# A row softmax on one core: the last two rows of the sixth tile's load move from Sync to GpSimd, behind a wait

## The chip, the cores and the metric

The kernel runs on one core of one Trainium2 chip. Time is the device time of one launch in microseconds; before the change it is 162.26 us, the median of three runs (162.25 to 162.98). Alongside stands one profiled execution, from which all durations below come.

## The reference

A softmax over the last axis of a float32 tensor of 16 x 1024 rows of 512 elements, at temperature 0.5:

```python
x_scaled = x / 0.5
x_max = np.max(x_scaled, axis=-1, keepdims=True)
exp_x = np.exp(x_scaled - x_max)
return exp_x / np.sum(exp_x, axis=-1, keepdims=True)
```

There are 16384 rows: 33.55 MB are read and 33.55 MB written.

## The kernel before, in words

**Tiles.** The rows are cut into eight tiles of 128 partitions x 16 rows x 512 elements (4 MB each). A partition's 16 rows lie next to each other in memory, so each partition's share of a tile is one run of 32 KB. Tiles are counted here as in the code, c = 0 to 7; "the sixth tile" is c = 5, "the fourth" c = 3. Six buffers hold tiles (`BUFS = 6`); tile 6 reuses the buffer of tile 0, tile 7 that of tile 1. Everything is done in place: the load writes the buffer, the exponentials overwrite it, the scaling overwrites it again, and the store reads it.

**Blocks.** Work on tiles goes by blocks (`BLOCKS`). Tile 0 is three blocks (rows 0-3, 4-7, 8-15), tiles 1 to 6 are one block each, tile 7 is two. So blocks 0, 1, 2 are tile 0, block 3 is tile 1, block 4 is tile 2, block 5 is tile 3, block 6 is tile 4, block 7 is tile 5, and there are eleven in all. `biases[5]` are therefore the biases of the fourth tile.

**Stages of a block.**
- `shift`: VectorE takes the negated maximum of each row (`tensor_reduce`, line 74) and doubles it (line 78); that is the bias. If the tile has no load yet, `shift` calls `load` first.
- `exponentials`: ScalarE computes exp(2x + bias) row by row, with the row's sum as a second output (line 85).
- `scale_vector`: VectorE takes the reciprocals of the sums (line 100) and multiplies seven eighths of the rows by them (line 102).
- `scale_scalar`: ScalarE scales the remaining eighth (line 111).
- `store`: ScalarE issues the store of the whole tile (line 119) after its last block.

**Order.** The order of each engine's instructions is the order in which the code calls them (`manual_schedule`). The main loop at lines 126 to 133 runs, for block i: exponentials of i+1, scaling of i, shift of i+2, store of i. So on VectorE the maximum of a block stands between the scaling of the block two before it and the scaling of the block one before it: the maximum of tile 5 (block 7) comes after the scaling of tile 3 (block 5) and before the scaling of tile 4 (block 6).

**Queues.** All loads are issued by Sync (line 66), in order of tiles. The first six tiles have a buffer of their own, so Sync issues their loads one after another at the start without a wait (the last, tile 5's, at 3.79 us). The loads of tiles 6 and 7 wait for the stores of tiles 0 and 1. All stores are issued by ScalarE. GpSimd has no work of the kernel. Waits between engines and on loads are put in from the buffers that instructions read and write.

Of the kernel before, what the change touches and what calls it, by code (L numbers as in the profile page):

```python
# [1 line left out]

# [4 lines left out]


@with_exitstack
def kernel(  # L10
    ctx: ExitStack,
    tc: tile.TileContext,
    x: bass.AP,
    out: bass.AP,
):
    nc = tc.nc
    fp32 = mybir.dt.float32
    P = nc.NUM_PARTITIONS
    AX = mybir.AxisListType.X
    EXP = mybir.ActivationFunctionType.Exp  # L20
    COPY = mybir.ActivationFunctionType.Copy
    MAX = mybir.AluOpType.max

    D = x.shape[-1]
    xf = x.flatten_outer_dims()
    of = out.flatten_outer_dims()
    N = xf.shape[0]

    G = 16
    C = N // (P * G)
    assert C * P * G == N
    xr = xf.rearrange("(c p g) d -> c p g d", p=P, g=G)
    outr = of.rearrange("(c p g) d -> c p g d", p=P, g=G)
    WHOLE = [(0, G)]
    LOADS = [[(0, 4), (4, G)]] + [WHOLE] * 7
    BLOCKS = [[(0, 4), (4, 8), (8, G)]] + [WHOLE] * 6 + [[(0, 8), (8, G)]]
    STORES = [WHOLE] * 8  # L40
    BMAX = 16
    BUFS = 6

    data = ctx.enter_context(tc.tile_pool(name="data", bufs=BUFS))
    stats = ctx.enter_context(tc.tile_pool(name="stats", bufs=6))

    ctx.enter_context(tc.manual_schedule())


    warm = stats.tile([P, 1], fp32, name="warm", bufs=1)  # L50
    nc.vector.memset(warm, 0.0)  # L51
    nc.scalar.activation(out=warm, in_=warm, func=EXP)  # L52

    chunks = {}
    blocks = [(c, lo, hi) for c in range(C) for lo, hi in BLOCKS[c]]
    n = len(blocks)
    biases, sums, recips = {}, {}, {}

    def load(c):
        if c < BUFS:  # L60
            chunks[c] = data.tile([P, G, D], fp32, name="xt")
        else:
            chunks[c] = chunks[c - BUFS]
        xt = chunks[c]
        for lo, hi in LOADS[c]:
            nc.sync.dma_start(out=xt[:, lo:hi, :], in_=xr[c][:, lo:hi, :])  # L66

    def shift(i):
        c, lo, hi = blocks[i]
        if c not in chunks:  # L70
            load(c)
        b = hi - lo
        negmax = stats.tile([P, BMAX], fp32, name="negmax")
        nc.vector.tensor_reduce(  # L74
            negmax[:, 0:b], chunks[c][:, lo:hi, :], axis=AX, op=MAX, negate=True
        )
        biases[i] = stats.tile([P, BMAX], fp32, name="bias")
        nc.vector.tensor_scalar_mul(biases[i][:, 0:b], negmax[:, 0:b], 2.0)  # L78

    def exponentials(i):  # L80
        c, lo, hi = blocks[i]
        sums[i] = stats.tile([P, BMAX], fp32, name="sums")
        for g in range(hi - lo):
            row = chunks[c][:, lo + g, :]
            nc.scalar.activation(  # L85
                out=row,
                in_=row,
                func=EXP,
                bias=biases[i][:, g : g + 1],
                scale=2.0,  # L90
                accum_out=sums[i][:, g : g + 1],
            )


    def scale_vector(i):
        c, lo, hi = blocks[i]
        b = hi - lo
        k = b - b // 8
        recips[i] = stats.tile([P, BMAX], fp32, name="recip")
        nc.vector.reciprocal(recips[i][:, 0:b], sums[i][:, 0:b])  # L100
        rows = chunks[c][:, lo : lo + k, :]
        nc.vector.tensor_mul(  # L102
            rows, rows, recips[i][:, 0:k].unsqueeze(2).broadcast_to((P, k, D))
        )

    def scale_scalar(i):
        c, lo, hi = blocks[i]
        b = hi - lo
        for g in range(b - b // 8, b):
            row = chunks[c][:, lo + g, :]  # L110
            nc.scalar.activation(  # L111
                out=row, in_=row, func=COPY, scale=recips[i][:, g : g + 1]
            )

    def store(i):
        c, _, end = blocks[i]
        for lo, hi in STORES[c]:
            if hi == end:
                nc.scalar.dma_start(
                    out=outr[c][:, lo:hi, :], in_=chunks[c][:, lo:hi, :]  # L120
                )

    shift(0)
    shift(1)
    exponentials(0)
    for i in range(n):
        if i + 1 < n:
            exponentials(i + 1)
        scale_vector(i)
        scale_scalar(i)  # L130
        if i + 2 < n:
            shift(i + 2)
        store(i)


# [1 line left out]
_INS = ['x']  # L137
_OUTS = [((16, 1024, 512), 'float32')]


# [23 lines left out]
```

## Time and profile before

| what | value |
|---|---|
| median of 3 runs | 162.26 us |
| profiled execution | 162.34 us |
| its span | 160.6 us |
| VectorE (DVE) busy | 134.6 us, 84% |
| ScalarE (ACT) busy | 102.1 us, 64% |
| GpSimd (POOL) busy | 0.2 us |
| mean DMA rate over the span | 418 GB/s |
| time to landing of the loads of tiles 0 to 5 | 4.9 and 11.7 (tile 0 in two pieces), up to 71.8 us (tile 5) |
| time to landing of a store, median | 22.8 us |

The span runs from the first to the last instruction that the profile shows; the rest of the time lies around it. A row of forty digits shows the busy share of forty equal slices of a stretch, in tenths. DMA queue q1 is Sync's, q10 ScalarE's, q14 the fetching of instructions. "Time to landing" is from the issue of a DMA to its last byte's arrival. A wait line reads: the engine, tile and line that waited, what it waited for, microseconds in total, how often, the longest. In lists in order of time the first two columns are start and duration in microseconds, and square brackets give idle time before an instruction and what ended it.

### The profile page before, as it was taken

To read this page: it belongs to the slowest core of one execution; us is meant where nothing else is said; L and a number is where in the kernel's file an instruction comes from. 1 tells how busy PE (TensorE), PEld (TensorE's weight loads), DVE (VectorE), ACT (ScalarE), POOL (GpSimd) and SP (SyncE) were. 2 spreads that over 40 slices of the span, in tenths; PEclk is the share of its full clock that TensorE was granted. 3 is DMA by queue.
4 is the path that set the end of the run, shared out by engine and by line. 5 is a ranking of instruction groups with operands and counts; after the bars stand their busy time and mean duration, and the time that the engine had idled before them with its cause. 6 is when DMAs were issued, how large, how long until landed. Compare 5 with 4: busy or idle time off the path is not lost.

```text
span 160.6 us, 402 instructions
## 1 busy us (share of the span) xinstructions
DVE 134.6 (84%) x45; ACT 102.1 (64%) x273; POOL 0.2 (0%) x4
## 2 busy tenths in 40 slices
DVE  0507999999999999999999999999999999957000
ACT  3071549069979963998199909991899891790000
POOL 0000000000000000000000000000000000000000
DMA  5999999999999999999999999999999999999993
GB/s 182 471 400 506 400 400 498 408 392 484 424 400 384 400 457 449 400 441 465 400 424 473 408 408 492 400 392 498 416 392 490 424 392 457 457 392 449 465 392 139
DMA packets 2450, 67.13 MB, mean 418 GB/s; under 512 B 272, under 2 KB 272, under 8 KB 272
## 3 DMA queue, kind: packets, MB, share of 16 engines
q1 hardware_dynamic: 1296, 33.56, 49.3%
q10 hardware_dynamic: 1152, 33.55, 48.4%
q14 instruction: 2, 0.02, 0.0%
HBM read 33.55 MB, written 33.55 MB: 418 GB/s over the span
## 4 chain that ended last, share of the span: by engine, by line
DVE 80%; DMA 7%; ACT 4%; issue 0%; SPq 0%
DVE negmax L74 42%; DVE xt L102 36%; DMA xt<-in_x_dram 7%; ACT xt L85 4%; DVE bias L78 1%; DVE recip L100 1%; SPq L66 0%
## 5 line engine op out<-in xcount | busy, mean ns | idle before, releaser
L85 ACT ACTIVATE xt<-xt,bias 128x512 f32<-128x512 f32 x128 | 90.4, 708 | 41.7 <-DVE bias L78 41.2
L74 DVE TENSOR_REDUCE negmax<-xt 128x16 f32<-128x8192 f32 (+2 forms) x11 | 69.9, 6352 | 9.5 <-DMA xt<-in_x_dram 9.5
L102 DVE TENSOR_TENSOR xt<-xt,recip 128x7168 f32<-128x7168 f32 (+2 forms) x11 | 62.0, 5637 | 0.4
L85 ACT ACTIVATION_READ_ACCUMULATOR xt<-xt,bias 128x1 f32 x128 | 23.9, 187 | 0.0
L111 ACT ACTIVATE xt<-xt,recip 128x512 f32<-128x512 f32 x15 | 9.9, 706 | 0.0
L100 DVE RECIPROCAL recip<-sums 128x16 f32<-128x16 f32 (+2 forms) x11 | 2.4, 218 | 1.8 <-ACT xt L85 1.8
L78 DVE TENSOR_SCALAR bias<-negmax 128x16 f32<-128x16 f32 (+2 forms) x11 | 1.9, 173 | 0.4
L52 ACT ACT_TABLE_LOAD x1 | 1.3, 1283 | 0.7 <-PEq L148 0.7
L51 DVE MEMSET warm<- 128x1 f32 x1 | 0.1, 59 | 0.8 <-PEq L148 0.8
L52 ACT ACTIVATE warm<-warm 128x1 f32<-128x1 f32 x1 | 0.2, 203 | 0.0
L148 POOL MEMSET const-bfloat16-1.0<- 128x1 bf16 x1 | 0.1, 103 | 0.0
L148 POOL MEMSET const-uint8-127<- 128x1 uint8 x1 | 0.1, 103 | 0.0
L148 POOL MEMSET const-float32-1.0<- 128x1 f32 x1 | 0.1, 100 | 0.0
L148 POOL MEMSET const-float32-0.0<- 128x1 f32 x1 | 0.1, 99 | 0.2 <-issue 0.2
## 6 DMA issues: line engine op xcount, KB each, us to landing
out_dram<-xt ACTq DMA_DIRECT2D x8, 4096.0 KB, 22.8
xt<-in_x_dram SPq DMA_DIRECT2D x7, 4096.0 KB, 30.2
xt<-in_x_dram SPq DMA_DIRECT2D x1, 3072.0 KB, 11.7
xt<-in_x_dram SPq DMA_DIRECT2D x1, 1024.0 KB, 4.9
```

Source lines behind the costliest of these rows:

```text
L51: nc.vector.memset(warm, 0.0)
L52: nc.scalar.activation(out=warm, in_=warm, func=EXP)
L74: nc.vector.tensor_reduce(negmax[:, 0:b], chunks[c][:, lo:hi, :], axis=AX, op=MAX, negate=True)
L78: nc.vector.tensor_scalar_mul(biases[i][:, 0:b], negmax[:, 0:b], 2.0)
L85: nc.scalar.activation(out=row, in_=row, func=EXP, bias=biases[i][:, g : g + 1], scale=2.0, accum_out=sums[i][:, g : g + 1],)
L100: nc.vector.reciprocal(recips[i][:, 0:b], sums[i][:, 0:b])
L102: nc.vector.tensor_mul(rows, rows, recips[i][:, 0:k].unsqueeze(2).broadcast_to((P, k, D)))
L111: nc.scalar.activation(out=row, in_=row, func=COPY, scale=recips[i][:, g : g + 1])
L148: nc = _bacc.Bacc("TRN2", target_bir_lowering=False, num_devices=1)
```

## The change

For the sixth tile alone (`SPLIT = 5`), Sync's load covers rows 0 to 13 of each partition. The last two rows (`TAIL = 2`) of all 128 partitions, 0.5 MB, are loaded by GpSimd instead, in two DMAs: partitions 126 and 127 first, then partitions 0 to 125. Ahead of them GpSimd copies one column of `biases[5]`, the biases of the fourth tile, into a small tile that nothing reads; since GpSimd works in order, its two DMAs are issued only after those biases exist. `max_dma_last_dim` limits the contiguous last dimension of a transfer; it is a number of bytes, here 4 x 512 = 2048, one row. Sync's loads are not held by any of this.

```diff
     STORES = [WHOLE] * 8
+    SPLIT, TAIL = 5, 2
+    HOLD = 5
     BMAX = 16
...
         xt = chunks[c]
         for lo, hi in LOADS[c]:
+            if c == SPLIT and hi == G:
+                hi = G - TAIL
+                hold = stats.tile([P, 1], fp32, name="hold", bufs=1)
+                nc.gpsimd.tensor_copy(hold, biases[HOLD][:, 0:1])
+                for p0, p1 in ((P - 2, P), (0, P - 2)):
+                    nc.gpsimd.dma_start(
+                        out=xt[p0:p1, hi:G, :],
+                        in_=xr[c][p0:p1, hi:G, :],
+                        max_dma_last_dim=4 * D,
+                    )
             nc.sync.dma_start(out=xt[:, lo:hi, :], in_=xr[c][:, lo:hi, :])
```

## The prediction

> **What bounds the kernel now.** I read the head of the page first: engines, the row of the DMA engines, the queues, the chain.
>
> ```profile
> span 160.6 us, 402 instructions
> DVE 134.6 (84%) x45; ACT 102.1 (64%) x273; POOL 0.2 (0%) x4
> DMA  5999999999999999999999999999999999999993
> ...
> q1 hardware_dynamic: 1296, 33.56, 49.3%
> q10 hardware_dynamic: 1152, 33.55, 48.4%
> q14 instruction: 2, 0.02, 0.0%
> ...
> DVE negmax L74 42%; DVE xt L102 36%; DMA xt<-in_x_dram 7%; ACT xt L85 4%; DVE bias L78 1%; DVE recip L100 1%; SPq L66 0%
> ```
>
> Two things are full at once. The sixteen DMA engines are busy 97.7% of the span (49.3 + 48.4), and the chain is VectorE from 12.88 us to 147.48 us. Neither can be lengthened for nothing, so I asked each for its slack. The waits from 13 us on hold nothing of a load after the second piece of tile 0; in order of time, around the change's two moments (the fourth tile's biases, the sixth tile's maximum):
>
> ```profile
> 62.80 0.17 DVE L78 TENSOR_SCALAR bias<-negmax 128x16 f32<-128x16 f32 x1
> 62.88 0.24 DVE L100 RECIPROCAL recip<-sums 128x16 f32<-128x16 f32 x1
> 63.01 0.72 ACT L85 ACTIVATE xt<-xt,bias 128x512 f32<-128x512 f32 x1 [4.01 <-DVE bias L78]
> 63.16 7.62 DVE L102 TENSOR_TENSOR xt<-xt,recip 128x7168 f32<-128x7168 f32 x1
> ...
> 87.32 8.68 DVE L74 TENSOR_REDUCE negmax<-xt 128x16 f32<-128x8192 f32 x1
> ```
>
> The biases are there at 62.97, and VectorE wants the whole sixth tile at 87.32: a window of 24.35 us. Before, that tile's load was issued at 3.79 and took 71.8 us, so it landed at 75.6, 11.7 us early. What does the DMA do in that window?
>
> ```profile
> DMA packets 352, 10.49 MB, mean 432 GB/s; under 512 B 32, under 2 KB 32, under 8 KB 32
> ## 3 DMA queue, kind: packets, MB, share of 16 engines
> q1 hardware_dynamic: 176, 5.24, 50.0%
> q10 hardware_dynamic: 176, 5.24, 50.0%
> ```
>
> This is 63.0 to 87.3 us. 352 less 32 small packets is 320 packets of 32 KB, 20 for each engine, so 24.3 / 20 = 1.215 us a packet, and loads (q1) and stores (q10) have exactly half each: one packet of one queue, then one of the other. Last, the end, 157.0 to 158.6 us in slices of 0.04 us, packets shown where they start:
>
> ```profile
> DMA  9999990900000000000000000000900000000000
> ```
>
> Fifteen engines have started their last packet by 157.3; one starts its last at 158.1, 0.8 us behind. It has done the same bytes as the others plus, I infer, the two instruction fetches of the q14 line (8 KB each; at 437/16 = 27.3 GB/s, 0.3 us each).
>
> The slack of the VectorE chain: the last store is issued at 147.55, takes 12.2 us, and its 4.19 MB alone need 4.19/437 = 9.6 us. With about 1.7 us for its start and receipt it would take 11.3 us on free engines, so a delay of VectorE has some 0.9 us of cover and after that moves the end one for one. From 87.32 to the end VectorE has no idle time but the 5.8 us for ScalarE at 137.56, which moves with it.
>
> **What the Trainium skill says.** "DMA: Bandwidth & Descriptors", Queues, rings and completion order: each engine goes round the queues that have work, one packet at a time. The half and half above agrees. The same page, SWDGE vs HWDGE vs iDMA: a GpSimd packet is preferably at most 4096 B; no trace here shows one. The same page, Why a DMA increments its semaphore by 16: a DMA runs on the largest number of engines up to 16 that divides its slowest dimension, on GpSimd as consecutive engines from a cursor, with an exception for some direct copies (all 16 engines, the partitions divided and rounded up). Not in this trace. "SBUF — State Buffer", SBUF: two separate sides: a VectorE operation with two SBUF inputs and a GpSimd operation that reads SBUF exclude each other; whichever is first keeps the ports for the whole instruction. Untested here.
>
> **The change, part by part.**
> *Sync's load* keeps its place but carries 14 rows: packets of 28 KB, 1.06 us (1.215 x 14/16). Nothing waits for it; it only lands earlier.
> *The hold copy* waits for VectorE's bias at 62.97. Nothing is queued behind it on GpSimd but the two new DMAs, and VectorE waits for nothing of GpSimd except the tail. Nearest row: GpSimd's 128x1 memsets, 0.10 us. ScalarE, which waits for the same bias, starts at 63.01, so the copy runs at about 63.05 to 63.2, and its rival for the port, the product of 63.16, has two inputs. I take the copy as first; VectorE then loses at most 0.1 us. If it loses, it runs at 70.78, 7.6 us later.
> *The two GpSimd DMAs*: no row. The page's first-byte price for a GpSimd DMA is about 1 us ("DMA: Bandwidth & Descriptors", Latency and other measured facts); two on one engine, 1 to 2.5 us, I take 1.5 as an estimate: about 64.7.
> *Engines.* By the divisor rule 2 partitions go to two engines and 126 to fourteen, nine each. If the exception holds, eight each. I take nine: the cap on the last dimension is in bytes, 4 x 512 = 2048, so each partition's 4 KB is two runs of one row. Two 2 KB runs fit one 4096 B packet, so nine packets an engine.
> *Turns.* Both other queues are full through the window: the sixth tile's load until about 73, the seventh's issued at 69.38, the stores of tiles 0 and 1. So each tail packet waits for one packet of each: 2 x 1.215 + 0.15 (4096 B at 27.3 GB/s) = 2.58 us a turn. The first waits up to a turn, more if engines are committed ahead: ScalarE's first store, issued at 45.58, started its packets at 49.6 to 50.9, against 0.9 us for the first load into empty queues. Bounds 0 to 4, taken 2.4. First packet 67.1; ninth eight turns later, 67.1 + 20.6 = 87.7, +0.15; the completion write behind it takes one more turn (0 to 2.58, taken 2.58) and receipt 0.4. Landing 90.8; bounds 85 to 93.
> *The wait.* VectorE's maximum of tile 5 waits for three landings instead of one. Two more waits cost some 0.04 us (22 ns each on SP's row of semaphores). The stall is 90.8 - 87.3 = 3.5 us. Queued behind it on VectorE are the sixth tile's biases and the product of tile 4; ScalarE's exponentials of tile 5 and all stores from tile 4 on come later by the same.
> *The end.* 3.5 less 0.9 of cover = +2.6 us. The relief of two light engines (7 partitions fewer, 28 KB, 1.03 us each) is worth nothing then, since the last store is issued after the queues have run dry; the fourteen get 4 KB more, 0.15 us, also hidden. Against the profiled execution, 160.6 span and 1.7 around it, 162.34 us: 164.9. Its distance to the median of 162.26 is nothing, and since the turn estimate leans on the late side of its bounds (a first turn caught early saves up to 2.4), I write 164.7.
>
> **The rivals.**
> *A, the tail travels in few packets.* If GpSimd puts an engine's whole share into one or two packets, it lands before 75 and VectorE never sees it. Then only the DMA's end counts: if the engine that is 0.8 us behind is one of the two light ones, it loses 1.03 us and the fourteen others, with 0.15 to 0.45 us more, set the end: 0.8 - 0.3 = 0.5 faster, 161.8. If it isn't light, up to 0.3 slower, 162.6. For it: the window of 24 us and no wait on loads in the middle. It decides from five packets an engine or fewer: 67.1 + 4 x 2.58 + 3.1 = 80.5. This one is not slower.
> *B* is the forecast, 163 to 166.6.
> *C, one row a packet.* 18 turns of 2.43 + 0.08 = 2.5 us: the last starts at 67.1 + 42.5 = 109.6, lands 112.6; stall 25.3, +24.4: 186.7. For it: each run of the trace's queues is a packet of its own. Against it: the page's 4096 B.
> *D, the hold copy loses the port* to the product of 63.16: all of B 7.6 us later, stall 11.1, +10.2: 172.5. For it: 0.1 to 0.15 us of margin, no more.
>
> **How the numbers follow.** Half a per cent, 0.8 us, is about what a measurement can tell from no change. A: 0.27 (same 0.20, faster 0.06, slower 0.01). B: 0.47, of which 0.05 end within 0.5% (first turn caught early, eight turns instead of nine). C: 0.16. D: 0.10. So slower 0.01 + 0.42 + 0.16 + 0.10 = 0.69, same 0.25, faster 0.06. B's own range is 162.9 to 166.6. The range has to take in A at its best, 161.5, and D, 173; C, 0.16, is left out.
>
> **What would show it.** In the profile after: an idle of VectorE before the sixth tile's maximum, put down to the DMA, of 1 to 5 us (B), some 11 (D), some 25 (C) or none (A); the times to landing of the two GpSimd issues, 26 us for the large one in B; a third queue with 126 x 1 + 2 data packets (B) or twice that (C). GpSimd's copy starts at 63.05, or in D at 70.8. The last store takes 11.3 us instead of 12.2 where VectorE was late. I am wrong if the third queue gets more than a packet a turn, or if the other queues leave turns free.

## The result and the profile after

The changed kernel takes 169.9 us (median of 4 runs, 169.46 to 169.97) against 162.31 us (4 runs): a ratio of 1.045, interval 1.042 to 1.049, 7.6 us slower. The profiled execution took 169.97 us with a span of 168.2 us.

The head of the page, the lines that answer to those of before:

```profile
span 168.2 us, 408 instructions
DVE 134.7 (80%) x45; ACT 102.1 (61%) x273; POOL 1.8 (1%) x7
DMA  5998989898989999999999989999998098985885
...
DMA packets 2642, 67.13 MB, mean 399 GB/s; under 512 B 336, under 2 KB 336, under 8 KB 464
...
q1 hardware_dynamic: 1296, 33.03, 46.8%
q10 hardware_dynamic: 1152, 33.55, 46.3%
q0 software_dynamic: 192, 0.52, 0.8%
...
xt<-in_x_dram POOLq DMA_DIRECT2D x1, 504.0 KB, 31.9
xt<-in_x_dram POOLq DMA_DIRECT2D x1, 8.0 KB, 9.8
```

VectorE does the same 134.7 us of work in a longer span. The third queue, q0, is GpSimd's: 0.52 MB in 192 packets, of which 464 - 336 = 128 lie between 2 and 8 KB, which at 512 KB in all are 4 KB each; the other 64 are of a few bytes. The small DMA needed 9.8 us to land 8 KB, the large one 31.9 us. In order of time, around the hold and around the sixth tile's maximum:

```profile
62.68 0.17 DVE L95 TENSOR_SCALAR bias<-negmax 128x16 f32<-128x16 f32 x1
62.92 0.18 POOL L76 COPY hold<-bias 128x1 f32<-128x1 f32 x1 [62.48 <-DVE bias L95]
63.04 1.48 POOL L78 DMA_DIRECT2D xt<-in_x_dram  x2
63.04 7.63 DVE L119 TENSOR_TENSOR xt<-xt,recip 128x7168 f32<-128x7168 f32 x1
...
95.72 8.69 DVE L91 TENSOR_REDUCE negmax<-xt 128x16 f32<-128x8192 f32 x1 [8.43 <-DMA xt<-in_x_dram]
```

The hold copy ran at once and both DMAs were issued by 64.5. VectorE then sat idle for 8.43 us, until 95.72, waiting for the tail. The chain of waits of the changed kernel has that landing on it:

```profile
63.74 31.90 DMA xt<-in_x_dram
95.64 0.03 DVEq L91
95.67 0.05 issue
95.72 8.70 DVE negmax L91
```

After it, VectorE's chain runs as before, and the last store, issued at 155.96 instead of 147.55, takes 11.1 us instead of 12.2: it finds free DMA engines. So the loss is one new wait, less a little cover at the end: 8.43 in, 7.6 out.

The forecast had this wait, but 3.5 us of it. Its data packets, their number and their size were as forecast. What was late? The DMA packets of the changed kernel from 66.0 to 72.2 us, when the forecast had the large DMA under way since 67.1:

```profile
DMA packets 126, 2.49 MB, mean 402 GB/s; under 512 B 42, under 2 KB 42, under 8 KB 44
...
q0 software_dynamic: 28, 0.01, 0.6%
```

GpSimd's queue had 28 packets there and moved next to nothing: two of 4 KB (44 - 42), the two partitions of the small DMA, and 26 of a few bytes. Some of these are completion writes, the packet of 4 bytes with which a DMA ends on every engine; the others, here called fillers, have 8 bytes and stand on engines for which the DMA has no data. That suggested theory T: the small DMA, which carries data on two engines only, still takes turns on all of them, and the large one stands behind it on the same rings.

### The profile page after: what moved, and what is told of

It reads as the page before. It is cut to its first block, busy times and chain, and to the rows that moved or that the text cites. A ratio compares the mean times of both kernels' runs of the same rounds, so it can differ in the third digit from the quotient of the medians.

```text
span 168.2 us, 408 instructions
## 1 busy us (share of the span) xinstructions
DVE 134.7 (80%) x45; ACT 102.1 (61%) x273; POOL 1.8 (1%) x7
## 4 chain that ended last, share of the span: by engine, by line
issue 37%; DVE 32%; DMA 19%; ACT 3%; POOL 0%; POOLq 0%; DVEq 0%
DMA xt<-in_x_dram 19%; DVE xt L119 16%; DVE negmax L91 15%; ACT xt L102 3%; DVE recip L117 0%; DVE bias L95 0%; POOL xt L78 0%; POOLq L176 0%; DVEq L91 0%; POOLq L165 0%
## 5 line engine op out<-in xcount | busy, mean ns | idle before, releaser
L102 ACT ACTIVATE xt<-xt,bias 128x512 f32<-128x512 f32 x128 | 90.4, 707 | 50.1 <-DVE bias L95 49.6
L78 POOL DMA_DIRECT2D xt<-in_x_dram x2 | 1.5, 744 | 0.0
## 6 DMA issues: line engine op xcount, KB each, us to landing
xt<-in_x_dram POOLq DMA_DIRECT2D x1, 504.0 KB, 31.9
```

Of the source, the lines that this page charges most:

```text
L78: nc.gpsimd.dma_start(out=xt[p0:p1, hi:G, :], in_=xr[c][p0:p1, hi:G, :], max_dma_last_dim=4 * D,)
L102: nc.scalar.activation(out=row, in_=row, func=EXP, bias=biases[i][:, g : g + 1], scale=2.0, accum_out=sums[i][:, g : g + 1],)
```

## Experiments

A turn is one packet of GpSimd's queue on an engine, with what the engine serves of the other queues before the next. Theory T: the landing is set by the number of turns. Each turn costs one packet of each other full queue, and the small DMA's filler and its completion write are turns too. Rival R: the small DMA is free on the other engines and the missing 4.9 us are a longer first wait or slow descriptors.

**The large DMA alone.** The 8 KB of the two partitions go to Sync.

```diff
-                for p0, p1 in ((P - 2, P), (0, P - 2)):
...
+                nc.gpsimd.dma_start(
+                    out=xt[0:P - 2, hi:G, :],
+                    in_=xr[c][0:P - 2, hi:G, :],
+                    max_dma_last_dim=4 * D,
+                )
+                nc.sync.dma_start(
+                    out=xt[P - 2:P, hi:G, :],
+                    in_=xr[c][P - 2:P, hi:G, :],
+                )
```

> As the change, but the two DMAs of GpSimd are one: partitions 0 to 125. The 8 KB of partitions 126 and 127 are loaded by Sync right ahead of its large load. Theory T (the small first DMA takes two turns on every engine, one for a data or filler packet and one for its completion write, and the large one queues behind it on the same rings): the first data of the large DMA starts 4.6 us after an issue at 63.1, the landing is 23.3 us later at 91.0 instead of 95.6, the stall of VectorE falls from 8.4 to about 3.8 us and the time to about 165.3 us. Rival R (the small DMA costs the other engines nothing, and the 4.9 us beyond the forecast are a longer first wait or slower turns): the landing is only about 0.6 us earlier, at 95.0, stall 7.8, time 169.2.

Measured: 165.85 us, ratio 1.021 (1.020 to 1.023). In the same stretch, 66.0 to 72.2 us, the queue now moves data:

```profile
q0 software_dynamic: 20, 0.07, 2.9%
```

and the maximum of the sixth tile starts 4.1 us earlier:

```profile
91.64 8.69 DVE L94 TENSOR_REDUCE negmax<-xt 128x16 f32<-128x8192 f32 x1 [4.30 <-DMA xt<-in_x_dram]
```

Landing at 91.6 against 91.0 forecast by T and 95.0 by R. As the account of the whole, R falls; a longer first wait has a part in the sum, as the section on the prediction shows.

**One GpSimd DMA of all 128 partitions.**

```diff
-                for p0, p1 in ((P - 2, P), (0, P - 2)):
+                for p0, p1 in ((0, P),):
```

> As the change, but one GpSimd DMA of all 128 partitions, so eight partitions for each engine instead of nine on fourteen. T: two turns of the small DMA and one data turn are gone, landing at 91.0 - 2.6 = 88.4, stall about 1.2 us, of which about 0.8 is covered: 162.7 us. R: one data turn and the earlier issue are gone: landing 92.4, stall 5.2, time 166.6.

Measured: 163.19 us, ratio 1.005 (1.003 to 1.006).

```profile
89.03 8.69 DVE L91 TENSOR_REDUCE negmax<-xt 128x16 f32<-128x8192 f32 x1 [1.59 <-DMA xt<-in_x_dram]
```

Another 2.6 us earlier, as T had it: one data turn fewer, eight partitions an engine instead of nine. The three kernels also measure the cover at the end: stalls of 8.43, 4.30 and 1.59 us became 7.6 (169.9 - 162.31), 3.5 (165.85 - 162.37) and 0.8 (163.19 - 162.37). The difference is 0.8 each time.

**Half-length packets on the other queues.** The change itself, with Sync's and ScalarE's transfers cut to runs of 16 KB.

```diff
             nc.sync.dma_start(
                 out=xt[:, lo:hi, :], in_=xr[c][:, lo:hi, :],
+                max_dma_last_dim=16384,
             )
...
                 nc.scalar.dma_start(
                     out=outr[c][:, lo:hi, :], in_=chunks[c][:, lo:hi, :],
+                    max_dma_last_dim=16384,
                 )
```

> As the change, hold and all, with the loads of Sync and the stores of ScalarE cut to runs of 16 KB, so that their packets are half as long (0.61 instead of 1.21 us). T (the tail waits for one packet of each other queue in every turn): a turn is 2 x 0.61 + 0.16 = 1.38 us, the large DMA lands about 18 us after its issue, near 81, no stall, about 162.8 us. A rival in which GpSimd's own descriptors or the memory are slow, whatever the others send: landing stays near 95 and the time near 169.9 us.

Measured: 163.03 us, ratio 1.005 (1.003 to 1.006). The same bytes by the same three queues, in more packets, and the tail lands in 18.6 us instead of 31.9:

```profile
q1 hardware_dynamic: 2320, 33.03, 48.7%
q10 hardware_dynamic: 2176, 33.55, 48.5%
q0 software_dynamic: 192, 0.52, 0.8%
...
xt<-in_x_dram POOLq DMA_DIRECT2D x1, 504.0 KB, 18.6
xt<-in_x_dram POOLq DMA_DIRECT2D x1, 8.0 KB, 6.5
```

VectorE starts the maximum at 87.45 with no wait. GpSimd's part was untouched, so neither its descriptors nor the memory made the landing late: the neighbours' packets set the length of a turn. They do not set the wait for the first packet: that came 4.4 us after the issue, against 4.7 in the changed kernel. It is also a remedy of 6.9 us in two arguments, though not one that beats the kernel before.

**More and fewer bytes by GpSimd.** Four rows and one row, otherwise the change.

```diff
-    SPLIT, TAIL = 5, 2
+    SPLIT, TAIL = 5, 4
```

> As the change, with TAIL = 4: 8 KB for each partition. If packets are at most 4 KB, 18 data turns: landing 95.6 + 9 x 2.63 = 119, somewhat earlier where the other queues run dry meanwhile (116 to 119), stall about 30, time about 191 us. If a packet holds a partition's whole share, nine turns of 2.73: landing 96.5, stall 9.3, 170.8 us.

Measured with four rows: 191.3 us (one run). 624 - 368 = 256 packets of 4 KB, twice as many, and a stall of 29.7 us, against about 30 forecast:

```profile
117.05 8.69 DVE L91 TENSOR_REDUCE negmax<-xt 128x16 f32<-128x8192 f32 x1 [29.70 <-DMA xt<-in_x_dram]
```

No packet holds more than 4 KB, though a partition's share is 8 KB here and 4 KB in the change (in rows of 2 KB both times).

```diff
-    SPLIT, TAIL = 5, 2
+    SPLIT, TAIL = 5, 1
```

> As the change, with TAIL = 1: one row, 2 KB for each partition, by GpSimd. It tells how GpSimd's packets are cut. If a packet never holds more than one partition's share, the nine turns stay, each only 0.08 us shorter: landing about 95.0, stall 7.8, 169.3 us. If packets are filled to 4 KB across partitions, five data turns remain: landing 95.6 - 4 x 2.63 = 85.1, no stall, about 162.8 us.

Measured with one row: 163.34 us (one run), no stall; the large DMA landed in 21.4 us. There are 65 packets between 2 and 8 KB for 256 KB, so two partitions' rows share a packet: packets are filled across partitions. The 0.5 us above the forecast I put down to the balance of the engines, below.

**Hold by an earlier tile: what is left without a stall.** Once with the order of the change and once, in the second edit on top of the first, with the two DMAs exchanged.

```diff
-    HOLD = 5
+    HOLD = 4
```

> As the change, but held by the biases of the third tile (about 46.1 us) instead of the fourth (62.7). T: the same number of turns, landing at about 79 us, 8 us before VectorE wants the tile, no stall. What is left is the balance of the DMA engines: 161.8 us if the engine that ended 0.8 us late in the kernel before is one of the two light ones, 162.5 if it is not. R (a longer wait or generation) also expects no stall. A rival that blames the GpSimd queue as such, wherever it is issued, expects some us of loss here too.

```diff
-                for p0, p1 in ((P - 2, P), (0, P - 2)):
+                for p0, p1 in ((0, P - 2), (P - 2, P)):
```

> As e3_hold4, with the order of the two GpSimd DMAs exchanged: partitions 0 to 125 first, then 126 and 127, which moves the two light engines to the other end of the round. No stall. Beside e3_hold4 it tells whether the late engine is a light one: the kernel in which it is light ends at 161.8, the other at 162.5; if it is light in neither, both at 162.5.

Measured: 162.78 us, ratio 1.002 (1.001 to 1.003), and 163.25 us, ratio 1.005 (1.004 to 1.007), where 161.8 and 162.5 were forecast. VectorE starts the sixth tile's maximum at 87.11 and 87.23, without a wait. The end of each kernel, 157.0 to 159.4 us in slices of 0.06, packets shown where they start: first `HOLD = 4`,

```profile
DMA  0009000009999999090000000000000000000000
```

then the exchanged order:

```profile
DMA  9000009099999900000090000000000009000000
```

With the change's order no engine is alone behind the others; with the order exchanged one starts its last packet at 159.0, 1.2 us after the bulk (up to 157.8, and one more at 158.2). That is what one expects if the engine that lagged in the kernel before is one of the two that the change makes light. That intention works. But the time does not follow: in the first row fourteen engines start their last packets at 157.5 to 158.1, later than the fifteen of before did (up to 157.3). The 28 KB packets took 1.108 us in the mean in this run instead of 1.06 in the changed kernel, eight of them on a heavy engine, and its nine 4 KB packets 0.16 us each: 8 x 1.108 + 9 x 0.159 = 10.3 us against 8 x 1.213 = 9.7 for the whole 32 KB packets, 0.6 us more. Beside it, the time from the last landing to the end of the span is about 0.3 us longer: 1.13 us against 0.85. There are more completions to wait for; that they are the cause is likely, but not tested. The late engine's gain is spent twice.

The pair also tests T a second time, and less well. With the large DMA in front it landed at 74.75 instead of 76.16, only 1.4 us earlier, though the small DMA's two turns (51.7 to 55.3 with the change's order) no longer stood ahead of it. GpSimd's queue from 51.5 to 52.1 us, first with the change's order, then exchanged:

```profile
q0 software_dynamic: 15, 0.00, 3.0%
```

```profile
q0 software_dynamic: 3, 0.01, 5.0%
```

With the small DMA in front fifteen engines have their first packet by then, with the large one three; the other thirteen follow at 53.6 to 54.6. So a small DMA in front costs its own turns, less what a large one waits longer for its first packet. Why that one waits longer, no run shows.

**Hold by the second tile, or none.**

```diff
-    HOLD = 5
+    HOLD = 3
```

> As the change, held by the biases of the second tile (about 33.2 us), when only Sync's loads are in flight. A turn is then one load packet and one of GpSimd, 1.21 + 0.16 = 1.37 us instead of 2.63, so the large GpSimd DMA lands in about 17 us instead of 32, near 51. No stall; time as with the hold one tile later, 162.8 us.

Measured: 162.91 us, ratio 1.005 (1.003 to 1.007), no stall; the large DMA landed in 22.5 us, not 17. I had again left out the small DMA ahead of it (6.7 us to land), and the stores, whose first packets come at about 50, joined before it was through.

```diff
-                hold = stats.tile([P, 1], fp32, name="hold", bufs=1)
-                nc.gpsimd.tensor_copy(hold, biases[HOLD][:, 0:1])
```

> As the change without the hold copy: GpSimd issues its two DMAs at the start. The tail then takes its turns among the packets of tile 0's second load, which lands up to 8 x 0.16 = 1.3 us later; VectorE's whole chain starts later by as much. 1.3 less the 0.8 of cover: 162.8 to 163.3 us. If the tail's early turns fall behind tile 0 (GpSimd slow to start), the time is that of the kernels held by earlier biases, 162.8.

Measured: 163.94 us, ratio 1.011 (1.009 to 1.012). The tail met tile 0's second load, and VectorE's second maximum waited 7.02 us instead of 4.78:

```profile
15.08 2.29 DVE L89 TENSOR_REDUCE negmax<-xt 128x4 f32<-128x2048 f32 x1 [7.02 <-DMA xt<-in_x_dram]
```

That is a start 2.2 us later, not 1.3; the 24 KB packets of that load took 1.03 us in the median (1.01 in the mean) instead of 0.91, eight of them 0.8 to 1.0 us more. So a hold is of use; for this tail the fourth tile's biases are too late, the second's and third's are not.

**A lighter version.** One row by GpSimd, in half rows, held by the third tile's biases.

```diff
-    SPLIT, TAIL = 5, 2
-    HOLD = 5
+    SPLIT, TAIL = 5, 1
+    HOLD = 4
...
-                        max_dma_last_dim=4 * D,
+                        max_dma_last_dim=2 * D,
```

> One row by GpSimd instead of two, cut to half rows (1024 bytes) so that the 126 partitions again go to fourteen engines, held by the third tile's biases. The late engine loses 7 x 2 KB, 0.5 us; the fourteen others gain five 4 KB packets for 8 x 2 KB, about 0.25 us: all engines end near 158.8 us instead of 159.4, and 0.3 us go to two more waits at the end of the kernel. 162.0 to 162.2 us, a gain too small to be told from none.

Measured: 162.36 us (13 runs) against 162.25 (17 runs), ratio 1.0003 (0.9995 to 1.0012): no gain, where 162.0 to 162.2 was forecast. Fifteen engines start their last packets within half a microsecond, and none later (same slices as above):

```profile
DMA  0009999999900000000000000000000000000000
```

The balance is what was sought. In the profiled execution the last landing comes 0.4 us earlier than before (159.31 against 159.71), and the end of the kernel takes 0.3 us of it back, where again 1.13 us follow that landing. No version that I ran beats the kernel before. One row in whole rows (`TAIL = 1` above, held by the fourth tile) kept a late engine:

```profile
DMA  0999999009900000000000000000000900000000
```

The counts of packets say why; first whole rows, then half rows:

```profile
DMA packets 2562, 67.13 MB, mean 416 GB/s; under 512 B 319, under 2 KB 319, under 8 KB 384
```

```profile
DMA packets 2578, 67.13 MB, mean 418 GB/s; under 512 B 328, under 2 KB 328, under 8 KB 400
```

Less the two data packets of the small DMA, the large one took 384 - 319 - 2 = 63 in whole rows and 400 - 328 - 2 = 70 in half rows. Nine rows of 2 KB on each of fourteen engines are four packets and a half, so five an engine: 70. All sixteen engines with eight rows, the last with six, are 15 x 4 + 3 = 63, and then one engine needs one filler: of the queue's 112 packets 112 - 65 - 32 completion writes - 14 fillers of the small DMA = 1 is left. So in whole rows the DMA ran on all sixteen engines and lightened none. This agrees with the exception in the Trainium skill, "DMA: Bandwidth & Descriptors", Why a DMA increments its semaphore by 16 and not by 1: on GpSimd some direct copies go to all sixteen engines, the partitions divided by 16 and rounded up. Which copies, the page does not say; here it was the one with a single run for each partition.

## Why the prediction was right or wrong

**Right: what bounds the kernel, and which rival.** VectorE's chain had 24.35 us of window and less than a microsecond of cover at its end. The wait came where B put it, in 126 + 2 packets of 4 KB. The last store on free engines was put at 11.3 us and took 11.1. The cover was put at 0.9 us and measured at 0.8, in part by luck: the store saved 1.1 us, and 0.3 us more passed between the last landing and the end (1.13 against 0.85), which the sum did not have. *Engines* was right with nine partitions on each of fourteen engines. A is out: packets are 4 KB, not an engine's share (by its own sum seven packets an engine, not five, would still have been in time: 67.1 + 6 x 2.58 + 3.1 = 85.7). C is out: two rows share a packet. D is out: the hold copy started at 62.92, the product at 63.04, 0.36 us after the start of the bias operation, exactly as before. The copy was still running then, by 0.06 us, so the exclusion that the Trainium skill describes in "SBUF — State Buffer", SBUF: two separate sides, did not show; so short an overlap does not settle it.

**Wrong: the size, 2.4 us forecast and 7.6 measured.** The step that failed is *Turns*: it let the large DMA's first packet go at 67.1 and put the small DMA ahead of it at nothing, without a reason. *Engines* had said "2 partitions go to two engines"; for the data that is so, but the other fourteen got packets too. GpSimd's queue did get its first turns from 67.8 on, but they were the small DMA's: on every engine a filler or a data packet, in the next turn the completion write, and only then, from 72.3 on, the large DMA's data. From 70 to 72 us, then from 72 to 74:

```profile
q0 software_dynamic: 15, 0.00, 0.4%
```

```profile
q0 software_dynamic: 29, 0.09, 11.1%
```

On ten of the fourteen engines the small DMA's two turns took about 4.5 us, from 67.8 to 68.3 until 72.3 to 72.9. The other four set the landing:

| four engines that ended last, start in us | forecast | measured |
|---|---|---|
| first packet of GpSimd's queue | 67.1 | 70.1 |
| first data packet of the large DMA | 67.1 | 73.6 |
| its ninth | 87.7 | 93.7 |
| its completion write | 90.4 | 95.1 |
| landing | 90.8 | 95.6 |

So their first turn came 3.0 us late, and the small DMA's two turns took 3.5 us; the eight turns between data packets took 0.5 us less than forecast, and the completion write came 1.3 us sooner after the data, with one long packet ahead of it instead of two. That is 4.7 of the 4.8 us. Two turns of 2.58 us added to the forecast, 90.8 + 5.2 = 96.0, come near the landing too, but in part by luck. The prediction's turn of 2.58 us has a load packet of 1.215 us in it, though until about 73 the load packets were the 28 KB ones that it had itself put at 1.06 us. And its own case of a first wait in a full queue, the 4 to 5.3 us of ScalarE's first store, fits the first packets at 67.8 to 68.3 better than the 67.1 that it took.

Taking the small DMA away moved the landing by 4.0 us: two turns fewer, but its own first packet came 5.9 us after the issue, against 4.7 for the small one's. Taking away one more turn moved it by 2.6. In the prediction's own terms the stall was 8.4 instead of 3.5, the cover nearly as written, the end 7.6.

I had counted the completion write of the large DMA as a turn and not that of the small one. What the Trainium skill says in "DMA: Bandwidth & Descriptors", Queues, rings and completion order, that an engine serves its queues one packet at a time, I applied to bytes and not to everything that a queue holds.

**Half right: the relief of two engines.** Rival A priced it at 0.5 us if the late engine is light. As far as the rows at the end show, the late engine is light and is relieved, but the fourteen others took 0.6 us longer instead of 0.15 to 0.45, and 0.3 us at the kernel's end were not in the sum at all. So A's better end did not exist: without a stall this change costs 0.2%.

## What to carry to other kernels

In these runs a small transfer on a queue of its own beside full queues was slow by its count of packets, not by its bytes: 504 KB took 31.9 us at 4 KB a turn behind two 32 KB packets, and 18.6 us behind two 16 KB ones. Count every packet of every DMA on that queue, completion writes and the fillers of engines with no data included, allow for a first wait of some microseconds, and ask whether the landing still fits before the consumer's start. Before relieving one engine of 1 us, price the packets added on all the others and the waits added at the end.

## What the runs showed of the hardware

- A GpSimd DMA of two partitions put a filler of 8 bytes on each of the fourteen engines that carried no data, and each took a turn. The DMA of 126 partitions did so on two engines, once for each of the others' nine packets: in the run with the large DMA alone, 160 packets less 126 with data less 16 completion writes are 18.
- GpSimd's packets were filled to 4 KB across partitions: 63 packets for 252 KB of 2 KB rows.
- Packet times were not only a matter of size. With the hold by the third tile GpSimd's 4 KB packets went between the 28 KB ones, and these took 1.11 us; held by the second tile, GpSimd's had gone by before, and they took 1.06. But with one GpSimd DMA of all partitions such packets went between the last 28 KB ones too (from 68.9 to 72.3 us), and all took 1.06. What lengthens them is open.
- Into two full queues the first packet of a GpSimd DMA came 4.7 us after its issue in the changed kernel, 4.4 us in the one with half-length packets, and 5.9 us in the one with the large DMA alone.
